# A direction's decay and rate latents in the two row halves of one tile, and both low-rank products issued together

## The chip, the core and the metric

The kernel runs on one core of a Trainium2 chip: five engines with queues of their own (TensorE for matrix products, VectorE, ScalarE, GpSimd, SyncE for issuing transfers), a state buffer of 128 partitions, and eight banks of accumulators that TensorE writes and VectorE and ScalarE read. The metric is the device time of one execution in microseconds (us); lower is better. The kernel before took 2045.86 us, the median of three runs (2044.41 to 2046.62).

## What is computed

The reference is one layer of a hybrid backbone over 256 latent tokens with 256 context tokens ahead of them, width 2048, in 32-bit floats. After a norm and a modulation, one input projection feeds two groups of heads. The part that matters here is the first group: 16 heads of width 64 with a recurrent state, run forward and backward. For each direction `d`, the decay and the rate `a` of every token come from low-rank latents of 64 columns:

```python
r, k, v, gd, wd_f, wd_b, ad_f, ad_b = _split_cols(q, RWKV_SIZES)
for d, (wd, ad) in enumerate(((wd_f, ad_f), (wd_b, ad_b))):
    w_log = -jax.nn.softplus(-(lp['rwkv_w0'][d] + jnp.tanh(wd) @ lp['rwkv_w_up'][d])) - 0.5
    decay = jnp.exp(-jnp.exp(w_log))
    a = jax.nn.sigmoid(lp['rwkv_a0'][d] + ad @ lp['rwkv_a_up'][d])
    kd = k * (1.0 + (a - 1.0) * lp['rwkv_k_a'])
    y, s_fin = _wkv7(rh, heads(decay), heads(kd), vh, kk, heads(a), s0, d == 1, want_output)
```

The second group is a diagonal state-space model (S5), also in both directions. Its output goes through a gated unit, both groups through one output projection, and a gated feed-forward block and a last norm follow.

## The kernel before, in words

Features lie on the partitions and all 512 tokens along the free axis. The program is fully unrolled; generators yield pieces of work in an order, and a scheduler then places the instructions of each engine's queue by priority and by its own estimate of when operands and buffers are ready. Each engine takes its queue in that order on the chip.

- *Start (to about 187 us).* Modulation, norm, and the first projection tiles in five banks. `lora` (line 452) makes the low-rank latents of all heads: `twd`, the decay latent after a hyperbolic tangent, with the forward direction in rows 0 to 63 and the backward one in rows 64 to 127, and `ad`, the rate latent, in the same way.
- *Head pairs beside the projection (to about 700 us).* `win_steps` and `win_quarter` (line 430: `ps_w<-hhi,hi` and the like) compute the rest of the input projection in tiles of 128 columns, each quarter 12 matmuls, whose weights ScalarE and VectorE split into two parts (lines 213, 214). `beside` steps through these and through `prepare`, in turn. For each of 8 head pairs `p`, `prep` loads the pair's low-rank weights `lup`, and for each direction `factors` computes the two low-rank products, lines 570 (decay) and 576 (rate), each into the single bank `l`, each read by one ScalarE activation (lines 572 into `sg`, 578 into `ta`), and then the factors on VectorE; `products`, woven with the next direction's `factors`, makes transpositions into bank `m` (lines 645, 689) and small products into banks `g` (line 663). After every two pairs `solve` inverts triangular blocks on GpSimd (lines 716, 718) and finishes them with small products in bank `m` (lines 736, 747).
- *Chains.* When all head pairs are done, `switch` closes those banks and opens others, and `chains(0)`, two recurrent chains of 8 steps each, starts beside what is left of the projection (lines 825, 826: 64-column products over 128 rows; 835: 64 x 64; 844, 845: over 128 rows; 866, 871: outputs). When the projection ends, the S5 inputs are loaded, and S5 runs beside `chains(1)`.
- *Output projection, gated unit, feed-forward (from about 1040 us, line 230).*

`self.apart()` (line 390) gives a group of TensorE instructions a high priority in the scheduler and states that its matmuls don't depend on each other. `bank(tag)` hands out the banks of a tag in turn: `l` has one, `g` and `m` have two each, `w` two, `d` one. In `beside`, one step of a projection tile is followed by 2 or 3 steps of `prepare`; a `yield` is such a step.

## Time and profile before

| | |
|---|---|
| median of three runs | 2045.86 us |
| the profiled execution | 2042.66 us |
| its span, first to last instruction | 2040.5 us |
| TensorE busy | 1875.2 us (92%) |
| VectorE busy | 1344.9 us (66%) |
| ScalarE busy | 883.7 us (43%) |
| mean granted TensorE clock | 0.931 |

In the profile's rows PE is TensorE's matmul, PEld its weight load, DVE VectorE, ACT ScalarE, POOL GpSimd, SP SyncE, and L570 is line 570 of the kernel. A matmul in 32-bit floats is two instructions (passes) in the trace, so 16 products show as x32. Tile names stand as out<-in without buffer numbers. A row of waits names the engine and line that waited, what released it, the us in total, the times and the longest. "Busy" counts an instruction until its modelled end, and the ends of matmuls overlap the next one's start, so for what a matmul costs the starts are compared.

### The profile page before, as it was taken

Reading aid. Unit: us, or ns where it says so; the run is one execution under the profiler, and the core shown is the slowest. Engines: PE = TensorE matmul, PEld = TensorE weight load, DVE = VectorE, ACT = ScalarE, POOL = GpSimd, SP = SyncE. Lnnn points to the kernel's source line nnn. Section 1 sums busy time; section 2 is a strip of 40 time slices with the busy share of each in tenths; the row PEclk is TensorE's granted clock in tenths of the full one; section 3 lists DMA queues with packets and bytes.
Section 4 is the critical chain, followed back from the end, with each engine's and each line's share of the span. In section 5 each row is a group of like instructions: output and inputs, shape, how many; then the busy total and the mean of one; then the engine's idle time right before and its main releaser. Section 6 shows DMA issues by size and latency. Waiting matters only on the chain.

```text
span 2040.5 us, 35440 instructions
## 1 busy us (share of the span) xinstructions
PE 1875.2 (92%) x13704; PEld 1451.1 (71%) x13704; DVE 1344.9 (66%) x2416; ACT 883.7 (43%) x1601; POOL 404.5 (20%) x625
## 2 busy tenths in 40 slices
PE   4898998998988999798988799999999999999997
PEld 1566765676766778565655577888888888888886
DVE  7625878748889463468688977766666666645544
ACT  2333554444544534242322354554555455544442
POOL 0301007037174450126575200000000000000000
PEclk9899998978888889788979899999999999999998
DMA  8882575733334756756478454666666665566664
GB/s 323 308 298 92 166 245 188 256 117 125 120 127 135 244 168 206 272 185 210 140 264 266 123 173 162 196 218 217 218 219 225 223 200 184 182 190 183 187 189 133
DMA packets 169816, 401.86 MB, mean 197 GB/s; under 512 B 25648, under 2 KB 60848, under 8 KB 165808
## 3 DMA queue, kind: packets, MB, share of 16 engines
q1 hardware_dynamic: 169648, 399.60, 59.6%
q8 instruction: 108, 1.77, 0.3%
q14 instruction: 60, 0.49, 0.1%
HBM read 357.98 MB, written 45.74 MB: 198 GB/s over the span
## 4 chain that ended last, share of the span: by engine, by line
PE 69%; DVE 11%; DMA 7%; POOL 3%; issue 3%; ACT 2%; SPq 0%; DVEq 0%; ACTq 0%; POOLq 0%
PE ps_w L230 27%; PE ps_m L230 12%; PE ps_w L430 9%; PE ps_d L379 3%; PE ps_g L663 2%; DMA modw<-modw_in 2%; DMA raw<-win_in 2%; PE ps_t L430 1%; PE ps_c L835 1%; PE ps_s L230 1%; POOL TM L718 1%; POOL tmp L716 1%; PE ps_v L430 1%; DMA own<-own 1%; PE ps_s L1328 1%
## 5 line engine op out<-in xcount | busy, mean ns | idle before, releaser
L220 DVE TENSOR_TENSOR lo<-raw,hi 128x1024 fp32r<-128x1024 f32 (+1 forms) x327 | 374.9, 1147 | 224.1 <-ACT hi L219 220.6
L219 ACT ACTIVATE hi<-raw 128x1024 fp32r<-128x1024 f32 (+1 forms) x327 | 322.4, 987 | 305.4 <-PE ps_w L230 222.3
L230 PE MATMUL ps_w<-h,hi 128*128 128x512 f32 x688 | 248.6, 400 | 0.3 <-DVE h L1517 0.3
L230 PE MATMUL ps_m<-h,hi 128*128 128x512 f32 x688 | 247.1, 398 | 1.8 <-ACT hi L219 1.8
L230 PE MATMUL ps_w<-hid,hi 128*128 128x512 f32 x704 | 247.6, 398 | 0.0
L230 PE MATMUL ps_w<-hid,lo 128*128 128x256 f32 x704 | 195.1, 281 | 0.0
L430 PE MATMUL ps_w<-hhi,lo 128*128 128x512 f32 (+2 forms) x448 | 177.6, 397 | 13.9 <-DVE lo L214 13.8
L230 PE MATMUL ps_m<-h,lo 128*128 128x256 f32 x688 | 187.2, 282 | 1.2 <-DVE lo L220 1.2
L230 PE MATMUL ps_w<-h,lo 128*128 128x256 f32 x688 | 186.5, 281 | 0.4 <-DVE lo L220 0.4
L214 DVE TENSOR_TENSOR lo<-raw,hi 128x512 fp32r<-128x512 f32 (+1 forms) x144 | 105.0, 732 | 117.5 <-ACT hi L213 113.8
L213 ACT ACTIVATE hi<-raw 128x512 fp32r<-128x512 f32 (+1 forms) x144 | 89.0, 620 | 211.0 <-PE ps_w L430 81.6
L430 PE MATMUL ps_w<-hhi,hi 128*128 128x512 f32 (+2 forms) x448 | 174.0, 389 | 5.8 <-ACT hi L213 5.8
L430 PE MATMUL ps_w<-hlo,hi 128*128 128x512 f32 (+2 forms) x448 | 171.2, 382 | 0.0
L230 PEld LDWEIGHTS ps_w<-h,hi 128*128 128x128 f32 x688 | 129.2, 188 | 40.8 <-ACT up L238 10.9
L230 PEld LDWEIGHTS ps_w<-hid,hi 128*128 128x128 f32 x704 | 131.3, 188 | 31.4
L230 PEld LDWEIGHTS ps_m<-h,hi 128*128 128x128 f32 x688 | 129.4, 188 | 29.8 <-ACT hi L219 2.6
L230 PEld LDWEIGHTS ps_w<-hid,lo 128*128 128x128 f32 x704 | 133.0, 189 | 1.5
L230 PEld LDWEIGHTS ps_m<-h,lo 128*128 128x128 f32 x688 | 129.9, 189 | 5.6 <-DVE lo L220 1.8
L230 PEld LDWEIGHTS ps_w<-h,lo 128*128 128x128 f32 x688 | 129.9, 189 | 3.6 <-DVE lo L220 0.7
L430 PEld LDWEIGHTS ps_w<-hhi,lo 128*128 128x128 f32 (+1 forms) x448 | 90.8, 203 | 48.2 <-DVE lo L214 21.7
L430 PEld LDWEIGHTS ps_w<-hhi,hi 128*128 128x128 f32 (+1 forms) x448 | 90.8, 203 | 30.0 <-ACT hi L213 12.9
L716 POOL TENSOR_TENSOR tmp<-AU,TM 128x31 f32<-128x31 f32 (+15 forms) x124 | 82.4, 664 | 128.6 <-DVE AU L707 119.7
(392 smaller groups left out, 3631.0 us busy)
## 6 DMA issues: line engine op xcount, KB each, us to landing
raw<-wup_in SPq DMA_DIRECT2D x176, 512.0 KB, 4.3
modw<-modw_in SPq DMA_DIRECT2D x152, 512.0 KB, 4.9
raw<-wdn_in SPq DMA_DIRECT2D x80, 512.0 KB, 3.5
raw<-win_in SPq DMA_DIRECT2D x140, 256.0 KB, 3.9
own<-own SPq DMA_DIRECT2D x32, 1024.0 KB, 5.5
modw<-modw_in SPq DMA_DIRECT2D x80, 256.0 KB, 3.9
own<-own SPq DMA_DIRECT2D x32, 640.0 KB, 3.9
raw<-wout_in SPq DMA_DIRECT2D x38, 256.0 KB, 3.8
```

Of the source, the lines that this page charges most:

```text
L213: nc.scalar.activation(out=hi, in_=raw, func=AF.Copy)
L214: nc.vector.tensor_tensor(out=lo, in0=raw, in1=hi.bitcast(F32), op=ALU.subtract)
L219: nc.scalar.activation(out=hi, in_=src, func=AF.Copy)
L220: nc.vector.tensor_tensor(out=lo, in0=src, in1=hi.bitcast(F32), op=ALU.subtract)
L230: mm = self.nc.tensor.matmul(out, lhsT=a, rhs=b, start=(n == 0), stop=(n == last), skip_group_check=True)
L379: self.behind(nc.tensor.matmul(ps[32 * j:32 * j + 32, :], lhsT=self.silu[:, k], rhs=ws[j], start=(k < 4), stop=(k >= 12)))
L430: self.nc.tensor.matmul(out, lhsT=w[:, j], rhs=x[:, k, lo:T], start=(k == 4 * job["qs"][0] and n == 0), stop=(k == 4 * job["qs"][1] - 1 an ...
L663: mm = nc.tensor.matmul(pss[h][:, 128 * c:128 * c + w], lhsT=BK[hr, 4 * s + c], rhs=X[hr, c, x1:x1 + w], start=True, stop=True)
L716: nc.gpsimd.tensor_tensor(out=tv, in0=AU[:, s + 1:32, s:s + 1].to_broadcast([128, n, m]), in1=TM[:, s:s + 1, 0:m].to_broadcast([128, n, m] ...
L718: nc.gpsimd.tensor_tensor(out=TM[:, s + 1:32, 0:m], in0=TM[:, s + 1:32, 0:m], in1=tv, op=ALU.subtract)
L835: nc.tensor.matmul(U[q:q + 64, i], lhsT=pt[q:q + 64, :, 8 * i + n], rhs=Ws[q:q + 64, i], start=True, stop=True)
L1328: nc.tensor.matmul(ps[64 * par:64 * par + 64, g, i], lhsT=MB[:, g, i, 64 * par:64 * par + 64], rhs=self.U2[:, pos], start=True, stop=True)
```

## The change

The columns of the input projection are put in another order on the host, so that the first latent tile holds the forward direction's decay latent in rows 0 to 63 and its rate latent in rows 64 to 127, and the second tile the same for the backward direction; the low-rank weights `lup` are laid out to match. `lora` keeps one tile for each direction (`wa0`, `wa1`) and applies the hyperbolic tangent to its upper half only, so twice on 64 rows and not once on 128. `factors` issues both products of a direction inside `apart()`, the decay product (rows 0 to 63) into bank `l` and the rate product (rows 64 to 127) into one of the two banks `m`, then both activations, and has one `yield` less. Everything else is as it was.

```diff
--- before.py
+++ after.py
@@ -81,7 +81,7 @@
     A["cc"] = np.stack([c[0], c_ctx], -1).reshape(16, 128, 2).transpose(1, 0, 2)
     order = [0, 4, 1, 5, 2, 6, 3, 7] + list(range(8, 24))
     A["modw"] = mod_w[0].reshape(16, 128, 24, 512).transpose(2, 1, 0, 3)[order]
-    cols = [np.arange(3232, 3360), np.arange(3360, 3488), np.arange(3072, 3200)]
+    cols = [np.r_[3232 + 64 * d:3296 + 64 * d, 3360 + 64 * d:3424 + 64 * d] for d in range(2)] + [np.arange(3072, 3200)]
     for p in range(NP):
         a = np.arange(128 * p, 128 * p + 128)
         cols += [1024 + a, 2048 + a, a]
@@ -100,7 +100,8 @@
     }
     A["vec"] = np.concatenate([vec[n] for n in VEC], 1)
     A["con"] = _const()
-    A["lup"] = np.concatenate([rwkv_w_up[0].reshape(128, 8, 1, 128), rwkv_a_up[0].reshape(128, 8, 1, 128),
+    lup = np.stack([rwkv_w_up[0].reshape(2, 64, 8, 128), rwkv_a_up[0].reshape(2, 64, 8, 128)], 0)
+    A["lup"] = np.concatenate([lup.transpose(0, 2, 3, 1, 4).reshape(128, 8, 2, 128),
                                rwkv_g_up[0][:128].reshape(128, 8, 1, 128)], 2)
     A["lup2"] = rwkv_g_up[0][128:].reshape(32, 8, 128)
 
@@ -451,11 +452,12 @@
 
     def lora(self, ps0, ps1):
         nc = self.nc
-        self.twd = self.res.tile([128, T], F32, name="twd")
-        self.ad = self.res.tile([128, T], F32, name="ad")
-        self.shift(ps0, 0, self.twd)
-        nc.scalar.activation(out=self.twd, in_=self.twd, func=AF.Tanh)
-        self.shift(ps1, 1, self.ad)
+        self.wa = []
+        for d, ps in enumerate((ps0, ps1)):
+            t = self.res.tile([128, T], F32, name="wa%d" % d)
+            self.shift(ps, d, t)
+            nc.scalar.activation(out=t[0:64], in_=t[0:64], func=AF.Tanh)
+            self.wa.append(t)
 
     def win_steps(self, i, lo=0, wcols=128):
         done, part = self.parts.get(i, (0, None))
@@ -563,19 +565,17 @@
 
         nc, rp, P = self.nc, self.rp, self.pair[p]
         k, r, kk, lup = P["k"], P["r"], P["kk"], P["lup"]
-        rows = slice(64 * d, 64 * d + 64)
         seg = "p (s t) -> p s t"
         ch = "p (c t) -> p c t"
-        ps = self.bank("l")
-        nc.tensor.matmul(ps, lhsT=lup[rows, 0], rhs=self.twd[rows], start=True, stop=True)
+        ps = [self.bank("l"), self.bank("m")]
+        with self.apart():
+            for i, rows in enumerate((slice(0, 64), slice(64, 128))):
+                nc.tensor.matmul(ps[i], lhsT=lup[rows, d], rhs=self.wa[d][rows], start=True, stop=True)
         sg = rp.tile([128, T], F32, tag="sg", name="sg", bufs=1)
-        nc.scalar.activation(out=sg.rearrange(seg, s=2), in_=self.rev(ps, d), func=AF.Tanh, scale=0.5,
+        nc.scalar.activation(out=sg.rearrange(seg, s=2), in_=self.rev(ps[0], d), func=AF.Tanh, scale=0.5,
                              bias=self.w0h[:, 8 * d + p:8 * d + p + 1])
-        yield
-        ps = self.bank("l")
-        nc.tensor.matmul(ps, lhsT=lup[rows, 1], rhs=self.ad[rows], start=True, stop=True)
         ta = rp.tile([128, T], F32, tag="ta", name="ta", bufs=1)
-        nc.scalar.activation(out=ta.rearrange(seg, s=2), in_=self.rev(ps, d), func=AF.Tanh, scale=0.5,
+        nc.scalar.activation(out=ta.rearrange(seg, s=2), in_=self.rev(ps[1], d), func=AF.Tanh, scale=0.5,
                              bias=self.a0h[:, 8 * d + p:8 * d + p + 1])
         yield
         nc.vector.tensor_scalar(out=sg, in0=sg, scalar1=0.5, scalar2=0.5, op0=ALU.mult, op1=ALU.add)
```

The scheduler makes another order of this. Three places on TensorE follow; lines of the changed kernel below line 566 are one or two higher than before, and `wa_1489` is the forward tile, `wa_1496` the backward one.

TensorE at the first head pair, before: the decay product of the forward direction stands in the middle of a projection tile, and its rate product (line 576) follows 22 matmuls later.

```order
L430 MATMUL ps_w<-hhi,hi 128x256
L430 MATMUL ps_w<-hlo,hi 128x256
L570 MATMUL ps_l<-twd,lup 128x512
L430 MATMUL ps_w<-hhi,lo 128x256
L430 MATMUL ps_w<-hhi,hi 128x256
```

The same engine now, at the place where the projection goes on after the start:

```order
L431 MATMUL ps_t<-hhi,lo 128x256
L514 MATMUL ps_l<-con,sq 128x2 x4
L573 MATMUL ps_m<-wa_1489,lup 128x512
L573 MATMUL ps_m<-wa_1496,lup 128x512
L431 MATMUL ps_w<-hhi,hi 128x512
```

Both rate products of the pair, forward and backward, stand at the head, each in a bank `m`; the two decay products follow after 48 and after 72 projection matmuls.

TensorE at the seventh head pair (pair 6), before: the rate product alone, behind the transpositions of the values.

```order
L430 MATMUL ps_w<-hhi,hi 128x512
L645 MATMUL ps_m<-con,v 64x64 x16
L1187 MATMUL ps_d<-MCk,s5Bd 32x128 x4
L576 MATMUL ps_l<-ad,lup 128x512
L430 MATMUL ps_w<-hlo,hi 128x512
```

Now, behind the last products of the second triangular solve:

```order
L431 MATMUL ps_w<-hhi,lo 128x512
L747 MATMUL ps_m<-PT,FN 32x32 x5
L573 MATMUL ps_m<-wa_1496,lup 128x512
L747 MATMUL ps_m<-PT,FN 32x32
L573 MATMUL ps_l<-wa_1489,lup 128x512
L747 MATMUL ps_m<-PT,FN 32x32 x26
```

The rate product of the backward direction (bank `m`) and the decay product of the forward one (bank `l`) have moved into the solve's products, with one of these between them.

TensorE in the first chain group, beside the projection, before: the 16 matmuls of line 835 are both chains' together.

```order
L430 MATMUL ps_w<-hhi,lo 128x512
L747 MATMUL ps_m<-PT,FN 32x32 x32
L835 MATMUL ps_c<-Ws,PT 64x64 x16
L430 MATMUL ps_w<-hhi,hi 128x512
L430 MATMUL ps_w<-hlo,hi 128x512
```

Now, at the step at which one chain is at line 835 and the other at lines 825 and 826:

```order
L431 MATMUL ps_w<-hlo,hi 128x512
L835 MATMUL ps_c<-Ws,PT 64x64
L825 MATMUL ps_c<-ZE,own 64x64
L835 MATMUL ps_c<-Ws,PT 64x64
L826 MATMUL ps_c<-ZO,own 64x64
L835 MATMUL ps_c<-Ws,PT 64x64
L825 MATMUL ps_c<-ZE,own 64x64
L835 MATMUL ps_c<-Ws,PT 64x64
```

The two chains stand half a step apart, and their matmuls, over 64 and over 128 rows, alternate one by one.

## Rows read from the trace of the kernel before

**Rows 1.** The page: span, busy TensorE, and its slices of 51 us.

```profile
span 2040.5 us, 35440 instructions
PE 1875.2 (92%) x13704; PEld 1451.1 (71%) x13704; DVE 1344.9 (66%) x2416; ACT 883.7 (43%) x1601; POOL 404.5 (20%) x625
...
PE   4898998998988999798988799999999999999997
...
PEclk9899998978888889788979899999999999999998
```

**Rows 2.** Windows by stage: stretch, its length, busy (instructions), clock, DMA share, GB/s.

```profile
187.00:652.00 465.00, 418.92 (x3166) 308.58 (x3167) 367.07 (x663) 221.06 (x492) 163.78 (x215) 0.88 0.48 161
652.00:829.00 177.00, 169.73 (x1883) 137.74 (x1882) 89.34 (x161) 79.00 (x168) 52.85 (x75) 0.93 0.60 195
829.00:1038.00 209.00, 181.96 (x2084) 124.67 (x2083) 141.28 (x322) 65.91 (x146) 94.15 (x176) 0.81 0.65 219
```

**Rows 3.** Instructions by line: duration min/median/max in ns, first and last start.

```profile
L512 PE MATMUL ps_l<-con,sq x64: 165/251/374, 189.5 to 613.5; 128*128 128x2 f32 x64
...
L430 PE MATMUL ps_w<-hhi,lo x448: 276/389/988, 193.9 to 829.3; 128*128 128x512 f32 x103, 128*128 128x256 f32 x42, 128*32 128x256 f32 x5
...
L825 PE MATMUL ps_c<-ZE,own x256: 222/222/369, 701.7 to 1010.0; 128*64 128x64 f32 x128
```

**Rows 4.** Timeline of TensorE: end of the first chain group, start of the second.

```profile
849.81 0.22 PE L871 MATMUL ps_y<-own,ZE 128*64 128x64 f32 x1
849.82 0.22 PE L871 MATMUL ps_y<-own,ZO 128*64 128x64 f32 x1
...
871.75 0.42 PE L825 MATMUL ps_c<-ZE,own 128*64 128x64 f32 x2
```

**Rows 5.** The chain that ended last, behind the projection: start, us, what.

```profile
841.91 6.66 DMA U<-ud
...
848.59 5.88 DMA s5pw<-s5Ld
854.47 1.34 DVE MP L1310 x3
```

**Rows 6.** Timeline of TensorE around one decay product: start, us, instruction.

```profile
207.35 0.28 PE L430 MATMUL ps_w<-hhi,hi 128*128 128x256 f32 x1
207.47 0.28 PE L430 MATMUL ps_w<-hlo,hi 128*128 128x256 f32 x1
207.68 1.12 PE L570 MATMUL ps_l<-twd,lup 64*128 64x512 f32 x2
208.73 0.38 PE L430 MATMUL ps_w<-hhi,lo 128*128 128x256 f32 x1
```

**Rows 7.** Groups by line, 187 to 652: busy, mean ns | idle before, releaser.

```profile
L570 PE MATMUL ps_l<-twd,lup 64*128 64x512 f32 x32 | 18.4, 654 | 0.8 <-ACT ta L578 0.8
L576 PE MATMUL ps_l<-ad,lup 64*128 64x512 f32 x32 | 18.0, 642 | 3.3 <-ACT sg L572 3.3
```

**Rows 8.** Waits, 187 to 652: us in total, times, longest.

```profile
ACT ta L578 <- DVE BK L620: 5.3, 1, 5.3
...
PE ps_l L576 <- ACT sg L572: 3.3, 3, 1.5
...
PE ps_m L645 <- ACT own L690: 1.9, 1, 1.9
```

**Rows 9.** Timeline of ScalarE: the hyperbolic tangent of the latents.

```profile
182.97 0.63 ACT L457 ACTIVATE twd<-twd 128x512 f32<-128x512 f32 x1 [0.88 <-DVE twd L448]
```

**Rows 10.** Timeline of TensorE around a block of chain matmuls.

```profile
802.93 0.40 PE L430 MATMUL ps_w<-hhi,hi 128*128 128x512 f32 x1
803.16 0.39 PE L430 MATMUL ps_w<-hlo,hi 128*128 128x512 f32 x1
803.60 2.03 PE L835 MATMUL ps_c<-Ws,PT 64*64 64x64 f32 x32
805.56 0.50 PE L430 MATMUL ps_w<-hhi,lo 128*128 128x512 f32 x1
805.90 0.40 PE L430 MATMUL ps_w<-hhi,hi 128*128 128x512 f32 x1
```

**Rows 11.** Timeline of TensorE where chain matmuls of two shapes alternate.

```profile
817.83 0.73 PE L866 MATMUL ps_y<-own,S 64*64 64x64 f32 x16
818.49 0.33 PE L826 MATMUL ps_c<-ZO,own 128*64 128x64 f32 x2
818.75 0.44 PE L866 MATMUL ps_y<-own,S 64*64 64x64 f32 x4
819.12 0.33 PE L825 MATMUL ps_c<-ZE,own 128*64 128x64 f32 x2
...
820.38 0.27 PE L826 MATMUL ps_c<-ZO,own 128*64 128x64 f32 x1
```

**Rows 12.** Waits, 652 to 829: us in total, times, longest.

```profile
PE ps_m L736 <- DVE AU L729: 2.5, 1, 2.5
```

## The prediction, made before the changed kernel was run

> **What bounds the kernel now.** I read the page first, then the windows by stage, then the groups of instructions and the waits of the stretch that the change touches, and last the timeline of TensorE at a few places. The page shows TensorE busy 1875.2 of 2040.5 us and nearly never below 8 tenths in a slice [rows 1]. The windows tell the stages apart [rows 2]: from 187 to 652 us head-pair work and projection share TensorE (418.92 of 465 busy, VectorE 367.07); from 652 to 829 TensorE is busy 169.73 of 177, so 7.3 us idle; from 829 to 1038 nothing is full (TensorE 181.96 of 209 at clock 0.81, VectorE 141.28), so that stretch is made of waits. After 1263 come the feed-forward products, in which the order of both kernels differs little and nothing is changed. The last projection product starts at 829.3, the chain products run from 701.7 on [rows 3], and the first chain group's last product starts at 849.82 [rows 4]. What sets the time after 829 is the S5 branch, which can load its inputs only when the projection is done: the chain that ended last goes there through two transfers into the first VectorE work at 854.47 [rows 5].
>
> **The change, part by part.**
>
> *The products themselves.* There are 16 decay and 16 rate products before and after, of the same size. One takes TensorE 1.14 us: the projection product before it starts at 207.47, the one behind it at 208.73, and such a product alone steps 0.12 [rows 6]. 32 of these are 36.5 us, before and after, unless the two of a pair run side by side in the two row halves. The trace has TensorE's matmuls in the order of its queue, so they would have to stand next to each other. In the order they don't: the scheduler places each as soon as its bank is free, the rate product into a bank m long before the decay product gets the one bank l. Once (pair 6) a rate and a decay product stand with a single other matmul between them, and those belong to the two directions; at the start two rate products are neighbours, in the same row half. I count nothing for this.
>
> *Waits removed.* The rate product used bank l after the decay product and waited for ScalarE to empty it: 3.3 us of idle TensorE, and once 0.8 us the other way round [rows 7, 8]. With two banks these 4.1 us go: **-4.1**.
>
> *Waits added.* The rate product now takes one of the two banks m, and eleven of the 16 wait there for an eviction by ScalarE; behind it in TensorE's queue stand projection products. The nearest row is the transposition into bank m, of whose 16 groups (one for each pair and direction) one waited 1.9 us [rows 8]; I take the same for the 16 rate products: **+1.9**, with 0 and 16 x 1.9 = 30 us as bounds, of which the upper would need every product to wait that long. What is late next on ScalarE is the rate activation, which still waits for VectorE's last read of the old rate tile (5.3 us once [rows 8]). The pair's low-rank weights are also needed earlier, but at least 74 matmuls stand between the last use of the old ones and the first of the new in every pair: 0. The second hyperbolic tangent costs ScalarE one instruction of at most 0.63 us at 183 us [rows 9]; the first use stands behind the first head sums, which start at 189.5 [rows 3]: 0, or +0.6 if that cover is gone.
>
> *Work moved.* The generator yields once less per direction, so head-pair work ends after fewer projection products: the first chain product stands behind 1404 projection matmuls, counting the whole queue, where it stood behind 1440. 36 x 0.23 us (the step of one, [rows 10]) = 8.2 us go from before the chains to beside them, which is nothing in the sum. But two things come with it. First, at the last projection product both chains of the first group have finished all 8 steps, where each had 7 (counted by line 835): 88 more chain matmuls, 176 passes, stand before it. A pass takes 0.041 to 0.061 us [rows 10, 11]; at 0.04, since half of them run two abreast, that is **+7.0** before 829 and as much less behind it. Second, the two chains no longer go in step, and their matmuls of 64 and of 128 rows alternate singly in the queue. I counted where neighbouring matmuls have another tile shape: 54 before and 50 now up to the first low-rank product, 265 and 286 from there to the first chain product, 69 and 167 from there to the last projection product, 378 and 333 behind it. What one costs: around a block of 32 chain matmuls the step from the projection product to it is 0.44 instead of 0.23 and the one behind it 0.34 instead of 0.23, so 0.21 and 0.11, mean **0.16** [rows 10]. In a stretch where they alternate, two passes of one and four of the other take 0.63 us a round (818.49 to 820.38, three rounds) where 0.23 would do; that is 0.20 a change [rows 11]. I take 0.16, with 0.11 and 0.20 as ends. So up to the chains 17 x 0.16 = **+2.7**, and beside the projection 98 x 0.16 = **+15.7**.
>
> The Trainium skill, TensorEngine Tiling (Array Packing), Key Properties, says that a change of the tiling mode drains TensorE. Had each change to wait for the whole pass in flight (0.22 us in [rows 4]), the 115 changes up to the last projection product would cost 25 instead of 18.4 us and the sum would come out 7 us higher; the rows show less than that drain.
>
> *A wait that goes.* TensorE stood 2.5 us for the last triangular solve [rows 12]. That solve now has more chain work in front of it: **-2.5**, or 0.
>
> The last projection product thus comes -4.1 + 1.9 + 2.7 + 7.0 + 15.7 - 2.5 = **20.7 us later**. That stage has 7.3 us of idle TensorE in 177, so there is nothing to hide it in.
>
> *What comes back.* Behind it the rest of the first chain group is gone: 849.82 - 829.3 = 20.5 us [rows 3, 4]. If the chains were what bounds the stretch to 1038, all of it would come back; if the S5 branch is, next to nothing, since its transfers start with the end of the projection and last to 854.47 [rows 5], longer than the chain's rest, which lies in their shadow. TensorE and VectorE are shared, so some does: I take half, **-10**, with 0 and -20.5 as ends.
>
> The sum is +10.7 us on the profiled execution's 2042.66 us (its span of 2040.5 and 2.2 around it): 2053.4. The median shown, 2045.86, is 3.2 above that execution, so I predict **2056.6**.
>
> **The rivals.**
>
> *No change:* the chains' lead comes back nearly whole (-18). Then +2.7, 2048.6. For it: from 829 to 1038 no engine is full [rows 2], and the second chain group starts only when the first is done. Against it: the S5 transfers in the chain that ended last [rows 5].
>
> *Faster:* a change of shape costs only 0.11 and the whole lead comes back: -4.1 + 1.9 + 1.9 + 7.0 + 10.8 - 2.5 - 20.5 = -5.5, 2040.4; with the solve and bank waits falling kinder, down to 2033. Here the sum of small waits in the 465 us of head-pair work, 46 us of idle TensorE [rows 2], also counts: a different order can move some of it either way.
>
> *Faster, by doing what the diff describes:* if the two products did run side by side, a pair would cost between 1.14 and 1.7 instead of 2.28 us (the lower with all passes abreast, the upper with one of four pass lengths saved), so 16 x 0.55 to 1.14 = 9 to 18 us less, and without the rest 2028 to 2037. The order speaks against it.
>
> The Trainium skill, same page, The Problem and Theoretical Speedup, promises up to twice the speed where the contraction is at most 64 rows, as it is here; by it the pair would cost 1.14 us and the kernel take 2028. It holds only for matmuls that meet in the queue.
>
> *Much slower:* a change costs 0.20, nothing of the lead comes back and the bank m waits take three times their price: -4.1 + 5.7 + 3.4 + 7.0 + 19.6 - 2.5 = +29, 2075. It decides once the S5 transfers begin as late as the projection ends, which the rows suggest.
>
> **How the numbers follow.** What a measurement of this kernel can tell from no change is about 0.2%, 4.1 us. I give the forecast (slower by 5 to 18 us) 0.38, much slower 0.09, no change 0.27, faster by a cheap alternation 0.23, faster by pairing 0.03. So faster 0.26, same 0.27, slower 0.47. Cases of both signs hold much of the chance: the forecast's own range is 2050 to 2064; the range for 8 in 10 runs from 2034, which takes in most of the faster cases, to 2069.
>
> **What would show it.** In the profile of the changed kernel the last projection product should start near 850 instead of 829.3, and the first S5 product as much later; the chain products should start some 8 us earlier than 701.7, and the first chain group should be finished when the projection ends. TensorE's wait for the decay activation should be gone. The decay and rate products should still take some 1.1 us each, one by one. I am wrong if the projection ends within 8 us of 829 (then the changes of shape are cheap or hidden), or if it ends late and the S5 products start no later (then the lead was worth all of it), or if the waits of the head-pair stage moved by more than 10 us, which I take as unchanged.

## The result, and the profile of the changed kernel

The changed kernel takes 2075.31 us (median of four runs, 2071.09 to 2084.49), the kernel before 2045.13 beside it: ratio 1.0153, 95% interval 1.0116 to 1.019. I had forecast 2056.6 and a range up to 2069; slower was right, the size was not. The profiled executions are 2084.49 and 2042.66 us, 41.8 apart; that of the changed kernel is the slowest of its four, so the account below adds up to more than the medians' 30.

The page of the changed kernel, for [rows 1]: TensorE is busy 30 us longer for the same 13704 passes, and the row of its granted clock (PEclk, in tenths of full speed) dips in the sixth and seventh slices (260 to 364 us).

```profile
span 2082.7 us, 35428 instructions
PE 1905.6 (91%) x13704; PEld 1471.5 (71%) x13704; DVE 1350.4 (65%) x2416; ACT 886.7 (43%) x1602; POOL 410.1 (20%) x625
...
PE   4898998998996999978987889999999999999997
...
PEclk9999977998998999978988799999999999999998
```

Windows between five marks show where: the first head sums, those of the fourth head pair, the first chain product, the last projection product, the first feed-forward product. First before, with other ends than [rows 2], then after; columns as there.

```profile
189.50:346.90 157.40, 148.76 (x979) 106.43 (x979) 122.85 (x241) 74.64 (x165) 40.46 (x55) 0.92 0.55 183
346.90:701.70 354.80, 317.79 (x2680) 241.08 (x2678) 269.78 (x469) 174.57 (x388) 137.77 (x186) 0.86 0.47 158
701.70:829.30 127.60, 122.38 (x1391) 98.98 (x1392) 61.40 (x108) 49.78 (x106) 38.39 (x51) 0.96 0.59 189
829.30:1263.60 434.30, 379.88 (x3610) 271.79 (x3609) 329.32 (x661) 149.83 (x294) 166.06 (x292) 0.86 0.61 201
```

```profile
194.60:357.80 163.20, 149.81 (x865) 105.92 (x865) 114.69 (x222) 71.59 (x159) 38.68 (x56) 0.79 0.44 149
357.80:717.20 359.40, 323.28 (x2772) 241.77 (x2772) 282.57 (x491) 176.35 (x392) 138.84 (x181) 0.91 0.50 167
717.20:881.40 164.20, 160.57 (x1591) 126.78 (x1591) 67.95 (x123) 55.09 (x113) 38.83 (x55) 0.94 0.49 151
881.40:1305.60 424.20, 362.40 (x3435) 262.63 (x3433) 323.86 (x643) 148.42 (x289) 171.81 (x292) 0.87 0.61 206
```

The length alone misleads, because each stretch holds another share of the projection. So I take its matmuls off, at 0.23 us each (512 columns, [rows 10]) or 0.12 (256, [rows 6]), 261.6 us in either kernel, and compare what is left, "beside the projection's own time".

| us beside the projection's own time | before | after | |
|---|---|---|---|
| before the first head sums | 189.5 | 194.6 | +5.1 |
| first three head pairs | 85.8 | 112.3 | **+26.5** |
| other five pairs | 231.0 | 223.2 | -7.8 |
| chains beside the projection | 61.3 | 89.7 | **+28.4** |
| from there to the feed-forward | 434.3 | 424.2 | -10.1 |
| the rest | 776.9 | 777.1 | +0.2 |

They add up to 42.3 us; the spans differ by 42.2. The first row is chance: TensorE's order is the same there, and other kernels with that start have 190.0 to 194.4. Two executions with one and the same order (before and e1 below) differ by 3 us in the first three pairs, 10 in the other five, 1 in the chains and 4 behind them, so the two bold rows ask for a cause; the -10.1 stands out less clearly.

The first three pairs. Their windows say what was lost: idle TensorE rose from 157.4 - 148.76 = 8.6 to 163.2 - 149.81 = 13.4 us, by 4.8. The clock fell from 0.92 to 0.79. What a stretch would save at full speed is estimated as its length times 1 less the clock, its "clock share" from here on: 12.6 us before and 34.3 after, so 21.7 more. 4.8 + 21.7 = 26.5, the whole difference; that it fits to a tenth is luck, since the clock's two decimals alone leave some 1.5 us open. The other five pairs got 17 us back (clock 0.86 before, 0.91 after: a share of 49.7 and of 32.3) and are yet only 7.8 quicker. The stretches of 20 us show the place, before:

```profile
280.00:300.00 20.00, 19.75 (x199) 15.89 (x199) 11.02 (x32) 10.05 (x26) 0.00 (x0) 0.91 0.74 246
300.00:320.00 20.00, 18.61 (x80) 10.66 (x79) 16.21 (x24) 8.60 (x18) 15.91 (x25) 1.00 0.79 275
```

and after:

```profile
280.00:300.00 20.00, 17.58 (x107) 12.98 (x105) 10.22 (x30) 9.91 (x23) 0.00 (x0) 0.66 0.61 220
300.00:320.00 20.00, 20.00 (x60) 11.39 (x59) 6.36 (x11) 3.28 (x8) 4.37 (x11) 0.50 0.33 119
```

TensorE looks full in the last row, but at the lower of its two levels, 1.2 GHz; it stood at that level for 34.1 us on end (286.3 to 320.4, clock 0.50). Its timeline there, where a low-rank product that took 1.12 us in [rows 6] takes 2.07, and projection matmuls step 0.43 instead of 0.23 until 320:

```profile
280.93 1.71 PE L663 MATMUL ps_g<-own,BK 64*128 64x128 f32 x16
282.57 0.79 PE L645 MATMUL ps_m<-con,vr 64*64 64x64 f32 x18
285.78 1.52 PE L380 MATMUL ps_d<-modw,silu 128*32 128x512 f32 x8 [2.42 <-DMA modw<-modw_in]
...
293.50 2.07 PE L573 MATMUL ps_m<-wa,lup 64*128 64x512 f32 x2
...
298.12 0.63 PE L431 MATMUL ps_w<-hhi,hi 128*128 128x512 f32 x1
298.54 0.63 PE L431 MATMUL ps_w<-hlo,hi 128*128 128x512 f32 x1
...
321.22 0.40 PE L431 MATMUL ps_w<-hlo,hi 128*128 128x512 f32 x1
321.46 0.40 PE L431 MATMUL ps_w<-hhi,lo 128*128 128x512 f32 x1
```

Ahead of the fall stand small head-pair products and waits, and few projection matmuls: at the third pair's first product only 200 were done where there had been 266, at the fourth's 290 instead of 380. The waits of these three pairs, after; they add up to 13.2 of the 13.4 us (the 4.5 us that the view also gives for VectorE's `r` end where the stretch begins, at the first head sums):

```profile
PE ps_g L663 <- DVE BK L620: 6.8, 6, 2.9
...
PE ps_d L380 <- DMA modw<-modw_in: 2.4, 1, 2.4
PE ps_l L514 <- ACT sq L544: 2.1, 1, 2.1
PE ps_w L431 <- ACT hi L214: 1.9, 2, 1.0
```

TensorE stood before small products for VectorE (BK, 6.8 us), where the whole head-pair stage before has:

```profile
PE ps_g L663 <- DVE BK L620: 0.2, 1, 0.2
```

The low-rank products themselves wait for nothing, unlike in [rows 7] (columns as there, 192 to 717 us):

```profile
L573 PE MATMUL ps_m<-wa,lup 64*128 64x512 f32 x32 | 22.5, 797 | 0.0
...
L573 PE MATMUL ps_l<-wa,lup 64*128 64x512 f32 x32 | 18.0, 641 | 0.0
```

Marks for [rows 3]: the chains begin 15.5 us later and the projection ends 52.1 us later.

```profile
L431 PE MATMUL ps_w<-hhi,lo x448: 274/389/796, 201.1 to 881.4; 128*128 128x512 f32 x103, 128*128 128x256 f32 x42, 128*32 128x256 f32 x5
...
L825 PE MATMUL ps_c<-ZE,own x256: 222/222/369, 717.2 to 1046.0; 128*64 128x64 f32 x128
```

The chains beside the projection alternate as the order said; two to four passes and a change of shape take 0.26 us, for [rows 11]:

```profile
831.75 0.33 PE L866 MATMUL ps_y<-own,S 64*64 64x64 f32 x2
832.00 0.33 PE L871 MATMUL ps_y<-own,ZO 128*64 128x64 f32 x2
832.26 0.33 PE L866 MATMUL ps_y<-own,S 64*64 64x64 f32 x4
832.52 0.33 PE L871 MATMUL ps_y<-own,ZE 128*64 128x64 f32 x2
```

### The profile page after: what moved, and what is told of

It reads as the page before. It is cut to its first block, busy times and chain, and to the rows that moved or that the text cites. A ratio compares the mean times of both kernels' runs of the same rounds, so it can differ in the third digit from the quotient of the medians.

```text
span 2082.7 us, 35428 instructions
## 1 busy us (share of the span) xinstructions
PE 1905.6 (91%) x13704; PEld 1471.5 (71%) x13704; DVE 1350.4 (65%) x2416; ACT 886.7 (43%) x1602; POOL 410.1 (20%) x625
## 5 line engine op out<-in xcount | busy, mean ns | idle before, releaser
L431 PE MATMUL ps_w<-hhi,hi 128*128 128x512 f32 (+2 forms) x448 | 179.0, 399 | 5.6 <-ACT hi L214 5.4
```

Of the source, the lines that this page charges most:

```text
L431: self.nc.tensor.matmul(out, lhsT=w[:, j], rhs=x[:, k, lo:T], start=(k == 4 * job["qs"][0] and n == 0), stop=(k == 4 * job["qs"][1] - 1 an ...
```

## The experiments

Four edits make up the change: the layout, the second bank, the shorter generator and the group's priority. e1 to e4 do one alone, or leave one out. Of each edit the lines that matter are shown. Where two activations or the generator are named, their lines are those of `factors`. Each median has the kernel before measured beside it (2046.4 to 2051.6).

**e1, the layout alone** (`rows` gone, `lup` and latents as in the change):

```diff
-        nc.tensor.matmul(ps, lhsT=lup[rows, 1], rhs=self.ad[rows], start=True, stop=True)
+        nc.tensor.matmul(ps, lhsT=lup[64:128, d], rhs=self.wa[d][64:128], start=True, stop=True)
```

> The kernel before with the new layout alone: latents by direction, the hyperbolic tangent twice on 64 rows, but both products as before, one after the other in bank l with a yield between them, no group. The order of TensorE's queue keeps the same counts (68 changes of tile shape between the first chain product and the last projection product, 400 chain matmuls there). My theory (the order decides: changes of tile shape, chain work and head-pair waits): within 4 us of 2045. Rival (the layout itself costs, by the second tangent or by row halves that now read one tile): more than 5 us above it, and the first head sums later than 189.5 us by 3 or more, as in the changed kernel (194.6).

2044.66, ratio 0.9992 (0.9968 to 1.0015). The first head sums start at 194.4 and the time is still that of before: the layout has no cost that shows.

**e2, one yield less in the kernel before:**

```diff
-        yield
         ps = self.bank("l")
         nc.tensor.matmul(ps, lhsT=lup[rows, 1], rhs=self.ad[rows], start=True, stop=True)
```

> The kernel before with nothing but the yield between the two products taken out; layout, bank and activations as before. 139 changes of shape beside the projection where the kernel before has 68, 59 more in the head-pair stage, 56 more chain matmuls ahead of the last projection product. My theory (changes at 0.14 us, chain passes at 0.045, half of the lead comes back): last projection product about 23 us later, the time +13 us. Rival (the second bank, through waits in the head-pair stage, makes the loss): no more than +5 us, since the bank is not touched. Rival (any new order loses against this one): between +15 and +30.

2050.61, ratio 1.0003 (0.9983 to 1.0023): no difference, where I had expected +13. The projection ends 21 us later, near the 23 of the theory, but the other five pairs and what follows the projection came out shorter (224.0, 421.3).

**e3, only the second bank:**

```diff
-        ps = self.bank("l")
+        ps = self.bank("m")
         nc.tensor.matmul(ps, lhsT=lup[rows, 1], rhs=self.ad[rows], start=True, stop=True)
```

> The kernel before with nothing but the rate product moved from bank l to bank m; the yield, the layout and the activations as before. 151 changes beside the projection instead of 68, 14 more in the head-pair stage, 88 more chain matmuls ahead of the last projection product. My theory (changes and chain passes): last projection product about 21 us later, +11 us. Rival (the second bank makes the whole loss, by keeping a bank m from the transpositions): +25 to +30, with waits of the head-pair stage 10 us or more above the kernel before. Rival (the shorter generator makes it): within 4 us of 2045.

2054.78, ratio 1.004 (1.0023 to 1.0058), some +8: near my theory's +11, and no match for the whole loss.

**e4, the changed kernel without the group:**

```diff
-        with self.apart():
-            for i, rows in enumerate((slice(0, 64), slice(64, 128))):
-                nc.tensor.matmul(ps[i], lhsT=lup[rows, d], rhs=self.wa[d][rows], start=True, stop=True)
+        for i, rows in enumerate((slice(0, 64), slice(64, 128))):
+            nc.tensor.matmul(ps[i], lhsT=lup[rows, d], rhs=self.wa[d][rows], start=True, stop=True)
```

> The changed kernel without the group's priority: both banks, the layout and the shorter generator stay, the two products are scheduled like any other. 157 changes beside the projection (changed kernel 167, before 68), 286 in the head-pair stage (323, before 259), 480 chain matmuls ahead of the last projection product. My theory (changes and chain passes): 47 changes fewer than in the changed kernel, 6 us less than it, about 2069. Rival (the priority, which puts rate products far ahead into bank m, makes the head-pair stage's loss of some 18 us): 2055 to 2060. Rival (it does nothing): within 4 us of 2075.

2046.57, ratio 0.9998 (0.9973 to 1.0023), below every range that I had named. My first theory, the sum of changes of shape and chain passes, falls as the account of the whole: they are nearly all still there (157 changes, 480 chain matmuls), and the loss is gone. The chain stage still costs its 26 us (87.2 beside the projection's own time), but the first three pairs are back at 80.5 and the other five are quicker (215.3). Its first three pairs, other five and chain stage, columns as above:

```profile
192.80:342.30 149.50, 140.28 (x968) 100.99 (x968) 116.40 (x232) 72.56 (x159) 30.61 (x42) 0.96 0.58 196
342.30:686.20 343.90, 318.66 (x2700) 242.11 (x2700) 269.36 (x480) 176.99 (x397) 144.28 (x197) 0.86 0.48 163
686.20:837.30 151.10, 144.51 (x1542) 114.30 (x1542) 68.44 (x123) 51.32 (x107) 40.65 (x53) 0.95 0.49 157
```

So the loss hangs on the group's priority. The second theory was that the rate product, put far ahead, keeps a bank m: from its end to its activation the 16 rate products hold their banks 234 us in all (181 in e4, 36 before in bank l).

**e5 and e6, the priority on one of the two alone** (e6 has `ps[0]` inside and `ps[1]` outside the group):

```diff
+        nc.tensor.matmul(ps[0], lhsT=lup[0:64, d], rhs=self.wa[d][0:64], start=True, stop=True)
         with self.apart():
+            nc.tensor.matmul(ps[1], lhsT=lup[64:128, d], rhs=self.wa[d][64:128], start=True, stop=True)
```

> The changed kernel, with the group's priority on the rate product alone; the decay product is scheduled like any other. My second theory (the loss is the rate product set far ahead: it takes a bank m and keeps it until the rate activation can run, 234 us of bank time in the changed kernel, 181 without the group, and the transpositions wait): 2065 to 2080, head-pair stage (first head sums to first chain product) 515 us or more. Rival (changes of tile shape: 159 beside the projection, 339 in the head-pair stage, against 167 and 323 in the changed kernel): 2070 to 2076 as well. Rival (any new order comes out by chance): anywhere from 2040 to 2075.

> The changed kernel, with the group's priority on the decay product alone; the rate product is scheduled like any other. My second theory (the rate product's bank m): 2042 to 2050, the rate products keep their bank for 180 us or less. Rival (the priority as such makes the loss): 2065 or more. Rival (changes of tile shape: 133 beside the projection, 252 in the head-pair stage): about 2055, since 105 changes at 0.14 us are 15 us less than the changed kernel and half of it is lost again.

e5: 2086.52, ratio 1.0206 (1.0177 to 1.0235), slower than my theory's range. e6: 2027.14, ratio 0.9914 (0.9877 to 0.9952), faster than both kernels and than every range I had named. The rate product's priority costs 40 us (e5 over e4) or 48 (the changed kernel over e6); the decay product's gives 19 (e6 under e4) or 11 (the changed kernel under e5). But e6 keeps its banks 184 us, as long as e4.

**e7, rate product not ahead of its decay product:**

```diff
+        self.tc.add_manual_dep(mm[1].ins, mm[0].ins.name, mybir.DependencyInfo(mybir.DependencyClass.NoSync,
+                                                                          mybir.DependencyReason.DATA), reason="pair")
```

> The changed kernel, with one more dependency in the scheduler: the rate product may not be placed ahead of its decay product. Nine of the 16 pairs then stand next to each other in TensorE's queue, in different row halves and different banks. My second theory (the bank m): the rate product no longer takes its bank early, so 2040 to 2055. On the products: if two row halves run side by side, an adjacent pair takes 1.1 to 1.7 us instead of 2.3, 5 to 10 us in all; if they don't, 2.3. Rival (changes of tile shape: 148 beside the projection, 272 in the head-pair stage): about 2066.

2060.94, ratio 1.0071 (1.0045 to 1.0097), above the 2040 to 2055 of my second theory. Nine pairs stand together, and these run side by side. Timeline of TensorE: both start at once, and both are through in 1.06 us (261.34 to 262.40); further on one alone takes 1.05.

```profile
261.34 0.69 PE L574 MATMUL ps_l<-wa,lup 64*128 64x512 f32 x1
261.34 0.69 PE L574 MATMUL ps_m<-wa,lup 64*128 64x512 f32 x1
261.87 0.59 PE L574 MATMUL ps_l<-wa,lup 64*128 64x512 f32 x1
261.88 0.59 PE L574 MATMUL ps_m<-wa,lup 64*128 64x512 f32 x1
262.40 0.66 PE L692 MATMUL ps_m<-con,BK 128*128 128x128 f32 x4
...
266.41 1.12 PE L574 MATMUL ps_l<-wa,lup 64*128 64x512 f32 x2
267.46 0.39 PE L431 MATMUL ps_w<-hlo,hi 128*128 128x256 f32 x1
```

All 32 products take 25.2 us (38.3 in the changed kernel). The first three pairs are mended (89.4), the kernel still loses in the chains (83.7), and what it gets back there is small (431.8).

**e8, two rate tiles:**

```diff
-        ta = rp.tile([128, T], F32, tag="ta", name="ta", bufs=1)
+        ta = rp.tile([128, T], F32, tag="ta", name="ta", bufs=2)
```

> The changed kernel with two buffers for the rate tile (ta) in place of one, group and banks unchanged, so that the rate activation need not wait until VectorE has read the other direction's rate. My second theory (the bank m is kept by that wait): bank time of the rate products well below 234 us, time 2045 to 2058. Rival (changes of tile shape: 175 beside the projection, 259 in the head-pair stage, against 167 and 323): about 2066, the gain being 64 changes less in the head-pair stage. Rival (the bank's time doesn't matter): 2070 to 2080.

2052.54, ratio 1.0035 (1.0008 to 1.0061). The banks are held 11 us, the first three pairs come to 95.2. This agreed with the second theory, but e4 and e6 (181 and 184 us, no loss) and e7 (64 us, a loss) don't. What e5 and the changed kernel share is the place of the head pairs, and that became the third theory; e9 parts it from the second.

**e9, the rate product with its priority, but behind the projection matmul issued last:**

```diff
+        self.tc.add_manual_dep(mm[1].ins, self.lastwin.ins.name, mybir.DependencyInfo(
+            mybir.DependencyClass.NoSync, mybir.DependencyReason.DATA), reason="behind the projection")
```

> The changed kernel; its rate product keeps the group's priority but may not be placed ahead of the projection matmul issued last before it. The products of the third and fourth pair then begin behind 200 and 297 projection matmuls (changed kernel 200 and 290; without the group 288 and 369; before 266 and 380). Beside the projection there are 97 changes of shape and 408 chain matmuls, nearly as before (68, 400). My third theory (head-pair work that stands bunched, with few projection matmuls between, lets TensorE wait and its clock fall): the loss stays, half clock and waits in the first three pairs as in the changed kernel, 2058 to 2075. Rival (the rate product put far ahead is itself the harm): 2040 to 2050. Rival (the changes of shape and the chain work beside the projection make the loss): 2045 to 2050, as these are nearly back.

2065.09, ratio 1.0092 (1.0063 to 1.012). The banks are held 94 us only, the chains beside the projection cost 68.8, nearly as before, and the first three pairs still take 102.4, at clock 0.83:

```profile
190.00:344.80 154.80, 145.28 (x891) 104.46 (x892) 117.59 (x232) 72.57 (x161) 42.34 (x52) 0.83 0.50 166
```

The second theory falls here, the third holds.

**e10 and e11, the yield put back, with and without the group:**

```diff
+        yield
         ta = rp.tile([128, T], F32, tag="ta", name="ta", bufs=1)
```

> The changed kernel with the yield put back between the two activations, so the generator is as long as before; group and banks stay. Third and fourth pair behind 216 and 321 projection matmuls, 98 changes of shape and 488 chain matmuls beside the projection. My third theory (bunching in the first pairs): a loss, somewhat smaller than the changed kernel's, 2055 to 2070. Rival (the shorter generator makes the loss): 2042 to 2050. Rival (changes of shape): 69 fewer beside the projection, 49 fewer in the head-pair stage, 2058.

> As the last, and without the group's priority: layout, second bank and both products issued together, the generator as long as before. Third and fourth pair behind 288 and 364 projection matmuls; 74 changes of shape and 400 chain matmuls beside the projection, as before. My third theory: no bunching, so as fast as the kernel without the group or faster, 2030 to 2048. Rival (any order but the first loses, by chance): 2050 or more.

e10: 2068.71, ratio 1.0116 (1.0068 to 1.0163), first three pairs 105.8. e11: 2053.94, ratio 1.0016 (0.9985 to 1.0047), first three pairs 84.0. Its first three pairs are as expected, but its time is above my 2030 to 2048 and in the range of the rival (any order but the first loses, by chance); beside the kernel before it shows no difference.

**e12, the kernel before, its decay product in a group of its own:**

```diff
-        nc.tensor.matmul(ps, lhsT=lup[rows, 0], rhs=self.twd[rows], start=True, stop=True)
+        with self.apart():
+            nc.tensor.matmul(ps, lhsT=lup[rows, 0], rhs=self.twd[rows], start=True, stop=True)
```

> The kernel before with the group's priority on its decay product alone; one bank, old layout, both yields. Third and fourth pair behind 266 and 380 projection matmuls, as before; 80 changes beside the projection and 464 chain matmuls. In the changed kernel, priority on the decay product alone came out 19 us below no priority. If that is an effect of the decay product coming early (its activation starts the pair's longest chain on ScalarE and VectorE), it shows here too: 2028 to 2036. If it was the order's chance or needs the second bank: 2040 to 2052.

2044.5, ratio 0.9976 (0.9947 to 1.0005). An early decay product shows no gain by itself.

**e13 and e14, the pacing alone:** behind a step of the projection come half of `now` steps of `prepare` (one more and one less in turn where it is odd). e13 is the changed kernel with the numbers 16, 4, 32, 6; e14 is e6 with 12, 7, 36, 4.

```diff
-            for _ in range(rate // 2 + n % 2 * (rate % 2)):
+            now = rate if rate != rates[0] or n > 32 else 4 if n <= 16 else 6
+            for _ in range(now // 2 + n % 2 * (now % 2)):
```

> The changed kernel with another pacing and nothing else: in the first 16 steps of the projection 2 steps of head-pair work each, in the next 16 three, then 2 or 3 in turn as before. Third and fourth pair now begin behind 228 and 326 projection matmuls (changed kernel 200 and 290), 44 changes of shape and 352 chain matmuls stand beside the projection (167 and 488). My third theory (bunched head-pair work in the first pairs lowers the clock; changes of shape beside the projection come on top): first three pairs about 95 us beside the projection's own time (changed kernel 112, before 86), clock there 0.83 to 0.88, the time 2050 to 2062. Rival (the rate product's priority costs wherever the pairs stand): 2070 to 2080. Rival (only the shape changes and chain work count): 2040 to 2046.

> The fastest version so far (group's priority on the decay product alone, 2027), with another pacing and nothing else: in the first 12 steps of the projection 3 or 4 steps of head-pair work, in the next 24 two, then as before. Third and fourth pair now begin behind 250 and 320 projection matmuls instead of 288 and 369; 104 changes of shape and 432 chain matmuls beside the projection (133 and 416). My third theory: bunching comes back without any priority on the rate product, first three pairs 90 us or more beside the projection's own time (81), clock there below 0.92 (0.95), the time 2038 to 2055. Rival (only the rate product's priority harms): 2022 to 2032.

e13: 2063.86, ratio 1.0073 (1.0048 to 1.0098), first three pairs 95.5 at 0.87. e14: 2057.24, ratio 1.0044 (1.002 to 1.0068), 97.1 at 0.86. The first three pairs moved as expected in both, with the rate product's priority and without; the totals stand 2 us above my ranges. In e13 the rate products hold their banks 237 us, as long as in the changed kernel, another sign against the second theory.

**e15 and e16, the fastest version again, and with two rate tiles:**

> The fastest version so far once more, unchanged: layout, second bank, shorter generator, and the group's priority on the decay product alone. If its gain is of the order of its queue and not of the chip's mood: 2022 to 2032. If the first measurement was a lucky one: 2035 to 2046.

> The fastest version so far with two buffers for the rate tile. Third and fourth pair behind 290 and 379 projection matmuls (288 and 369), so no bunching either; 193 changes of shape beside the projection (133) and 323 in the head-pair stage (252), 416 chain matmuls (416). My third theory with changes at 0.14 us: 131 more changes are 18 us, of which some comes back: 2035 to 2045. Rival (the single rate tile is what holds the pairs up): below 2025. Rival (changes of shape cost next to nothing in all): 2025 to 2032.

e15: 2024.34, ratio 0.988 (0.9855 to 0.9904). e16: 2091.08, ratio 1.0212 (1.0176 to 1.0248), far off my 2035 to 2045, by the other five pairs (243.9) and the chains (111.0). Chains beside the projection, e15 and e16; the clock is 0.95 and 0.83:

```profile
695.30:833.00 137.70, 133.73 (x1403) 105.63 (x1403) 64.13 (x113) 49.21 (x103) 40.18 (x53) 0.95 0.55 171
```

```profile
723.90:901.10 177.20, 169.59 (x1409) 131.34 (x1408) 61.48 (x111) 51.48 (x104) 33.91 (x51) 0.83 0.43 137
```

**e17, e4 with two rate tiles; e18, e6 with the yield put back:**

> The changed kernel without the group's priority and with two buffers for the rate tile. Beside the projection it has the same 193 changes of shape and 416 chain matmuls as the last slow version (2091; there 111 us beside the projection's own time at clock 0.83), the head-pair stage 267 changes (323 there). Third and fourth pair behind 290 and 379 projection matmuls. My third theory with the changes as the chain stage's price: first three pairs below 92 us, chain stage 100 to 111 us beside the projection's own time, time 2055 to 2075. Rival (the second rate tile as such makes the loss): 2080 or more. Rival (that slow version was slow by the decay product's priority): 2045 to 2050.

> The fastest version (group's priority on the decay product alone, 2024) with the yield put back. Third and fourth pair behind 288 and 364 projection matmuls (288 and 369), 92 changes of shape beside the projection (133), 472 chain matmuls (416). My third theory: no bunching, first three pairs 80 to 86 us beside the projection's own time, chain stage 65 to 76, time 2020 to 2040. Rival (the shorter generator is part of the gain): 2045 or more.

e17: 2096.47, ratio 1.0209 (1.0144 to 1.0274). The chain stage cost 105.9, as expected, but the total missed, again by the other five pairs (244.5), and fell in the range of the rival that the second rate tile as such makes the loss. Against that rival stands e8, where the same edit took 23 us off the changed kernel. Other five pairs and chain stage of e17, to be held against e4's:

```profile
355.90:724.10 368.20, 338.29 (x2690) 256.73 (x2686) 265.97 (x471) 174.30 (x387) 135.84 (x186) 0.81 0.45 150
724.10:896.50 172.40, 164.58 (x1410) 127.69 (x1409) 61.36 (x105) 51.37 (x104) 37.24 (x52) 0.85 0.44 138
```

The clock share went from 48.1 to 70.0 us in the one and from 7.6 to 25.9 in the other, 40 of the 48 us by which these two stretches cost more beside the projection's own time. By this estimate it is again the granted clock that took the time; why it fell there, with the fourth pair behind 379 projection matmuls, no run shows. e18: 2032.94, ratio 0.9918 (0.9884 to 0.9952), as expected.

All orders in one table, in us beside the projection's own time, by where the fourth pair begins (the prediction counted 69 changes of shape before, not 68):

| | projection matmuls ahead of pairs 3, 4 | first three pairs (clock) | other five | chains (changes of shape) | to feed-forward | median |
|---|---|---|---|---|---|---|
| changed | 200, 290 | 112.3 (0.79) | 223.2 | 89.7 (167) | 424.2 | 2075 |
| e5 | 200, 290 | 114.0 (0.81) | 223.0 | 99.8 (159) | 417.6 | 2087 |
| e9 | 200, 297 | 102.4 (0.83) | 220.7 | 68.8 (97) | 434.4 | 2065 |
| e14 | 250, 320 | 97.1 (0.86) | 232.6 | 66.9 (104) | 431.2 | 2057 |
| e10 | 216, 321 | 105.8 (0.83) | 229.8 | 76.8 (98) | 425.5 | 2069 |
| e8 | 208, 323 | 95.2 (0.86) | 216.8 | 94.7 (175) | 416.7 | 2053 |
| e13 | 228, 326 | 95.5 (0.87) | 232.9 | 56.7 (44) | 448.9 | 2064 |
| e3 | 236, 332 | 89.0 (0.89) | 221.6 | 86.0 (151) | 421.4 | 2055 |
| e11 | 288, 364 | 84.0 (0.92) | 233.2 | 63.9 (74) | 439.8 | 2054 |
| e18 | 288, 364 | 84.9 (0.92) | 219.9 | 68.9 (92) | 425.5 | 2033 |
| e4 | 288, 369 | 80.5 (0.96) | 215.3 | 87.2 (157) | 424.4 | 2047 |
| e6, e15 | 288, 369 | 81.3, 84.5 (0.95, 0.94) | 219.5 | 78.7, 76.4 (133) | 414.7 | 2027, 2024 |
| e2 | 266, 372 | 84.1 (0.93) | 224.0 | 87.9 (139) | 421.3 | 2051 |
| e16, e17 | 290, 379 | 92.3, 92.1 (0.91, 0.92) | 243.9, 244.5 | 111.0, 105.9 (193) | 408.9, 426.2 | 2091, 2096 |
| before, e1, e12 | 266, 380 | 85.8, 82.5, 81.8 (0.92 to 0.96) | 231, 241, 249 | 61.3, 62.6, 72.5 (68, 68, 80) | 434, 430, 411 | 2046, 2045, 2045 |
| e7 | 282, 384 | 89.4 (0.89) | 222.1 | 83.7 (148) | 431.8 | 2061 |

The first three pairs take 102 to 114 us where the fourth begins behind fewer than 300 projection matmuls, 89 to 106 at 320 to 332, 80 to 92 at 364 and more, and the clock goes with it: with idle TensorE and the clock share taken off, these pairs come to 63 to 70 us in every one of the twenty kernels. The first three pairs of e9, e10, e13 and e14 were told in advance from the place alone. The chains go with their changes of shape: 57 to 69 us up to 104 changes (e10 and e12 above that), 76 to 79 at 133, 84 to 100 at 139 to 175. The 106 to 111 at 193 are not the changes' doing alone: the clock share is 30.1 us in e16 and 25.9 in e17, and without it and idle TensorE both cost 73 us, no more than the changed kernel's 76 at 167.

## Why the prediction was wrong, step by step

*The step that failed* is the head-pair stage, for which the prediction had -4.1 + 1.9 + 2.7 = +0.5 us and which cost 18.7: 26.5 more in the first three pairs, 7.8 less in the other five. It priced waits and changes of shape there and took the rest as unchanged; it had no term for the granted clock. The low-rank products wait for nothing, but their early place let three head pairs run ahead of the projection; there TensorE waited 4.8 us more and lost 21.7 by the clock, 34.1 us on end at half of it. My own sign of being wrong, waits that move by more than 10 us, would not have caught it: idle TensorE in the whole stage went from 45.6 to 49.5 us. I had read in the order that the rate products stand far ahead, and asked only what waits for their bank; I did not count how many projection matmuls were left between the head pairs, which the order shows as well (200 and 290 instead of 266 and 380).

*Products one by one, 36.5 us before and after:* right, 38.3, none side by side. My doubt about row halves was about the order, not the array, and e7 bears that out: adjacent they cost 1.06 a pair. Sixteen pairs would be worth some 16.6 us by that, within the 9 to 18 of that rival; in e7, with nine, the products cost 13 us less than in the changed kernel, and the kernel is still 0.7% slower than the one before.

*Waits removed, -4.1:* right, both rows of low-rank products show 0.0. *Waits added, +1.9:* none shows, neither there nor at bank m.

*Changes of shape and chain work:* I had +15.7 and +7.0, less 2.5 for a wait that goes, 20.2 beside the projection; it was 28.4, undersized by 8. The solve's wait went, and TensorE waited 2.4 us for a chain's eviction instead; idle TensorE fell by 1.6 us in all. The two prices were fair. An estimate for this stage from all twenty traces, with idle TensorE and the clock share taken off and a line fitted to changes and chain passes, gives 0.17 us a change and 0.04 a pass, and meets each trace within 3.5 us. What the sum lacked is here too the clock, 0.94 instead of 0.96 over a longer stretch: a share of 9.9 us where it had been 5.1. The last 2 to 3 us stay without an account. The +2.7 for the head-pair stage can't be told from chance.

*Half of the lead comes back, -10:* right in the way, since the first chain group ends with the projection (883.0 for 881.4) and the first S5 product came as much later as the projection's end, 51.8 us for 52.1. That the size, -10.1, meets it to a tenth is luck: half was a guess, and one order's two executions differ by 4 us in this stretch.

*Marks:* last projection product at 881.4, not 850; first chain product 15.5 us later, not 8 earlier, since the time lost ahead outweighed 36 matmuls.

*The rivals:* "much slower" had nearly the measured time (2075), but for other reasons: its three prices (bank waits, 0.20 a change, no lead) are not where the time went. "No change" is what e4 measures, the change without its group, but not by that rival's reason: there the chains still cost 26 us more, and the other five pairs were 16 quicker. What stays open is why single edits don't add: two rate tiles are worth -23 with the group and +50 without, 40 of it by the clock in the other five pairs and the chains.

## What to carry to other kernels

When a change moves small products ahead of a filler, count how much filler is left between them, stretch by stretch, before pricing waits: in this kernel it was there that TensorE waited and its clock fell. Few filler matmuls are not the only case (e17), so take the granted clock of each stretch into the account as well. Take the filler's own time off each stretch before comparing two profiles, and compare the same order twice to know the noise of a stretch. Try a group's priority on each of its products by itself: here the decay product alone, with both banks, gave 2027 and 2024 us in two measurements, 0.9 and 1.2% below the kernel before. Why it beats no priority at all (e4) by 19 us is not shown.

## What the runs showed of the chip that I had not expected

Two products in different row halves and banks, next to each other in the queue, started at the same time and took 1.06 us together, as one alone does (e7); I had expected them to be able to, not that nothing at all would be lost. And the mean clock of the whole execution says little: 0.931 before and 0.929 after, while the first three pairs went from 0.92 to 0.79 and cost 21.7 us by it; the other five, from 0.86 to 0.91, hid that in the mean.
